# A split GELU gate on one core: a small 16-partition load issued ahead of the first store on ScalarE's queue

## The chip, the core and the metric

The kernel runs on one core of a Trainium2 chip. The metric is the device time of one execution in microseconds (us), the median over the runs shown; lower is better. The core has engines that take their own instructions in order: ScalarE (ACT in the profile), VectorE (DVE), GpSimd (POOL), SyncE (SP), TensorE (PE). SP and ACT each feed a DMA queue (q1 and q10 in this profile), and 16 DMA engines move what both queues hold.

## What is computed

The input is split in two halves along its last dimension; the first half goes through the exact GELU and is multiplied by the second.

```python
x = np.random.randn(32, 512, 2048).astype(np.float32)
x1, x2 = x[..., :1024], x[..., 1024:]
out = (0.5 * x1 * (1 + erf(x1 / np.sqrt(2)))) * x2
```

134.22 MB are read and 67.11 MB are written, and each element is used once.

## The kernel before

The 16,384 rows are cut into 16 tiles of 1,024 rows: 128 partitions with 8 rows each. One tile's input takes 64 KB of each partition (8 MB in all), its output 32 KB (4 MB in all). There are two input buffers `x0`, `x1` and two output buffers `o0`, `o1`; tile i uses number i % 2.

Everything is ordered by hand, with semaphores. `load` (L49) issues a load on SP's queue. `store` (L56) waits until VectorE has done all multiplies issued so far (`mul_done`) and then issues a store on the queue that it is given. Ahead of the loop ScalarE issues `opening` (L63), a load of 512 bytes to each of 8 partitions of a scrap tile; SP issues the load of tile 0 in two halves of 4 rows (semaphores `first[0]` and `first[1]`) and that of tile 1 whole.

In the loop over tiles, each tile is worked in steps of rows: (0,5) and (5,8), and for the first and the last tile (0,2), (2,4) and (4,8). Each step is one GELU on ScalarE (L87), from the input buffer to the output buffer, and one multiply on VectorE (L95) in the output buffer. After the steps the store of the tile goes out on ScalarE's queue (q10) and the load of tile i + 2 on SP's (q1). Tile 0 is stored in two halves of 4 rows, 16 KB per partition each: the first half as soon as its second step is multiplied (`hi == 4`), the second at the end of the tile. The store of tile 14 and the two half stores of tile 15 go out on SP's queue instead, and count on `tail_stored`.

The load of tile i + 2 and the store of tile i count on the same semaphore, `ready[i % 2]`, 16 for each. ScalarE waits for it once ahead of a tile's first GELU, so that a tile begins when its input has landed and the store that last used its output buffer has landed too:

```python
            if i == 0 and lo % 4 == 0:
                nc.scalar.wait_ge(first[lo // 4], 16)
            elif lo == 0:
                nc.scalar.wait_ge(ready[k], n[ready[k].name])
```

At the end ScalarE waits for `opened` (the scrap load), and SP waits for `tail_stored` (L125), which is the last instruction.

Of the kernel before, what the change touches and what calls it, by code (L numbers as in the profile page):

```python
# [1 line left out]

# [4 lines left out]

GELU = mybir.ActivationFunctionType.Gelu


@with_exitstack
def kernel(
    ctx: ExitStack,
    tc: tile.TileContext,
    x: bass.AP,
    out: bass.AP,
):
    nc = tc.nc
    P = nc.NUM_PARTITIONS

    x_flat = x.flatten_outer_dims()
    out_flat = out.flatten_outer_dims()
    n_rows, dim = x_flat.shape
    half = dim // 2

    R = 8
    x_t = x_flat.rearrange("(n p r) d -> n p r d", p=P, r=R)
    o_t = out_flat.rearrange("(n p r) d -> n p r d", p=P, r=R)
    n_tiles = x_t.shape[0]
    x_bufs = [nc.alloc_sbuf_tensor(f"x{k}_tile", [P, R, dim], x.dtype) for k in range(2)]  # L30
    o_bufs = [nc.alloc_sbuf_tensor(f"o{k}_tile", [P, R, half], out.dtype) for k in range(2)]

    first = [nc.alloc_semaphore(f"first{j}") for j in range(2)]
    ready = [nc.alloc_semaphore(f"ready{k}") for k in range(2)]
    gelu_done = nc.alloc_semaphore("gelu_done")
    mul_done = nc.alloc_semaphore("mul_done")
    tail_stored = nc.alloc_semaphore("tail_stored")
    opened = nc.alloc_semaphore("opened")  # L40
    scrap = nc.alloc_sbuf_tensor("scrap_tile", [8, 128], x.dtype)
    n = {sem.name: 0 for sem in [*first, *ready, gelu_done, mul_done, tail_stored, opened]}

    def counted(ins, sem, by):
        ins.then_inc(sem, by)
        n[sem.name] += by

    def load(i, rows, sem):
        ins = nc.sync.dma_start(out=x_bufs[i % 2][:, rows, :], in_=x_t[i][:, rows, :])  # L49
        counted(ins, sem, 16)  # L50
        return ins

    def store(queue, i, rows, sem):
        queue.wait_ge(mul_done, n[mul_done.name])
        counted(
            queue.dma_start(out=o_t[i][:, rows, :], in_=o_bufs[i % 2][:, rows, :]), sem, 16  # L56
        )

    opening = nc.scalar.dma_start(out=scrap[:, :], in_=x_t[0][:8, 0, :128])  # L63
    counted(opening, opened, 16)
    for ins in (
        opening,
        load(0, slice(0, 4), first[0]),
        load(0, slice(4, 8), first[1]),
        load(1, slice(0, 8), ready[1]),
    ):  # L70
        tc.no_tile_sem_insts.add(ins.ins.name)
    tc.close()
    tc.compile()  # L73

    for i in range(n_tiles):
        k = i % 2
        last = i == n_tiles - 1
        pieces = i == 0 or last
        steps = ((0, 2), (2, 4), (4, 8)) if pieces else ((0, 5), (5, 8))
        for lo, hi in steps:  # L80
            rows = slice(lo, hi)
# [4 lines that stand above are left out]
            counted(  # L86
                nc.scalar.activation(  # L87
                    out=o_bufs[k][:, rows, :], in_=x_bufs[k][:, rows, :half], func=GELU
                ),
                gelu_done,  # L90
                1,
            )
            nc.vector.wait_ge(gelu_done, n[gelu_done.name])
            counted(
                nc.vector.tensor_mul(  # L95
                    out=o_bufs[k][:, rows, :],
                    in0=o_bufs[k][:, rows, :],
                    in1=x_bufs[k][:, rows, half:],
                ),
                mul_done,  # L100
                1,
            )
            if pieces and hi % 4 == 0:
                if last:
                    store(nc.sync, i, slice(hi - 4, hi), tail_stored)
                else:
                    store(nc.scalar, i, slice(hi - 4, hi), ready[k])
        if not pieces:
            if i == n_tiles - 2:
                store(nc.sync, i, slice(0, R), tail_stored)  # L110
            else:
                store(nc.scalar, i, slice(0, R), ready[k])
        if i + 2 < n_tiles:
            nc.sync.wait_ge(mul_done, n[mul_done.name])
            load(i + 2, slice(0, R), ready[k])


    nc.scalar.wait_ge(opened, 16)
    nc.scalar.drain()  # L119
    for sem in (*first, *ready, opened):  # L120
        nc.scalar.sem_clear(sem)
    nc.vector.drain()
    nc.vector.sem_clear(gelu_done)
    nc.sync.sem_clear(mul_done)
    nc.sync.wait_ge(tail_stored, n[tail_stored.name]).then_inc(  # L125
        tail_stored, -n[tail_stored.name]
    )


# [1 line left out]
_INS = ['x']  # L131
_OUTS = [((32, 512, 1024), 'float32')]


# [23 lines left out]
```

## Time and profile before

| | |
|---|---|
| time, median of 3 runs | 469.23 us (469.21 to 469.29) |
| profiled execution, first to last instruction (span) | 467.8 us |
| median less span, outside the first and last instruction | 1.4 us |
| VectorE busy | 140.5 us, 34 multiplies |
| ScalarE busy | 115.5 us, 34 GELUs and one table load |
| HBM traffic | 201.3 MB, 430 GB/s over the span |
| DMA packets | 5,057 |

The profile gives the profiled execution's span and no separate device time for it; the three timed runs lie within 0.08 us of one another. Times in the views are counted from the first instruction. "ACTq" and "SPq" mark DMA issues by ScalarE and SyncE, which are not counted as busy. The trace also holds one record for each DMA packet: its start, its queue, how long it took and its bytes. It does not name the DMA engine, but on one engine a packet begins when the one before it ends, so that the records can be strung together into 16 rows.

### The profile page before, as it was taken

The page shows a single profiled execution, that of the slowest core. Times are in us where ns is not written, and L with a number is a line of the kernel's source. Part 1 is how long each engine was busy: PE and PEld are TensorE (multiplying, and loading weights), DVE is VectorE, ACT ScalarE, POOL GpSimd, SP SyncE. Part 2 cuts the span into 40 slices and gives each one's busy share as a digit, 9 for nine tenths or more (in the row PEclk, how much of TensorE's full clock was granted, in tenths as well). Part 3 has the DMA queues.
Part 4 walks back from the last instruction along what each step waited for, and adds up shares of the span by engine and source line. Part 5 has one row for each costly group of instructions (what it writes and reads, how often), then busy time and mean ns, then how long its engine had stood idle before and what let it go on. Part 6 is the DMA issues. An engine that isn't in the chain of part 4 may idle for free.

```text
span 467.8 us, 154 instructions
## 1 busy us (share of the span) xinstructions
DVE 140.5 (30%) x34; ACT 115.5 (25%) x35; POOL 0.2 (0%) x4
## 2 busy tenths in 40 slices
DVE  0330515207051060511606115060150702507043
ACT  1320606041060410604105050050501506014060
POOL 0000000000000000000000000000000000000000
DMA  8999999999999999999999999999999999999988
GB/s 359 448 448 448 398 406 496 403 403 448 459 437 403 440 412 493 403 403 448 487 409 403 445 406 493 403 403 448 493 403 403 448 426 471 403 426 426 493 384 379
DMA packets 5057, 201.34 MB, mean 430 GB/s; under 512 B 568, under 2 KB 576, under 8 KB 576
## 3 DMA queue, kind: packets, MB, share of 16 engines
q1 hardware_dynamic: 2880, 142.61, 70.6%
q10 hardware_dynamic: 2176, 58.73, 29.1%
q14 instruction: 1, 0.01, 0.0%
HBM read 134.22 MB, written 67.11 MB: 430 GB/s over the span
## 4 chain that ended last, share of the span: by engine, by line
DMA 76%; DVE 14%; ACT 8%; ACTq 0%; SPq 0%; issue 0%
DMA out_dram<-o_tile 66%; DVE o_tile L95 14%; DMA x_tile<-in_x_dram 10%; ACT o_tile L87 8%; ACTq L119 0%; SPq L49 0%
## 5 line engine op out<-in xcount | busy, mean ns | idle before, releaser
L95 DVE TENSOR_TENSOR o_tile<-o_tile,x_tile 128x5120 f32<-128x5120 f32 (+3 forms) x34 | 140.5, 4171 | 319.7 <-ACT o_tile L87 319.7
L87 ACT ACTIVATE o_tile<-x_tile 128x5120 f32<-128x5120 f32 (+3 forms) x34 | 114.3, 3407 | 337.3 <-DMA out_dram<-o_tile 301.8
L87 ACT ACT_TABLE_LOAD x1 | 1.3, 1283 | 2.9 <-PEq L73 2.9
L142 POOL MEMSET const-bfloat16-1.0<- 128x1 bf16 x1 | 0.1, 102 | 0.0
L142 POOL MEMSET const-uint8-127<- 128x1 uint8 x1 | 0.1, 101 | 0.0
L142 POOL MEMSET const-float32-0.0<- 128x1 f32 x1 | 0.1, 99 | 0.2 <-issue 0.2
L142 POOL MEMSET const-float32-1.0<- 128x1 f32 x1 | 0.1, 98 | 0.0
## 6 DMA issues: line engine op xcount, KB each, us to landing
out_dram<-o_tile ACTq DMA_DIRECT2D x13, 4096.0 KB, 44.7
x_tile<-in_x_dram SPq DMA_DIRECT2D x2, 4096.0 KB, 16.7
out_dram<-o_tile ACTq DMA_DIRECT2D x2, 2048.0 KB, 34.4
out_dram<-o_tile SPq DMA_DIRECT2D x1, 4096.0 KB, 25.2
out_dram<-o_tile SPq DMA_DIRECT2D x2, 2048.0 KB, 7.8
x_tile<-in_x_dram SPq DMA_DIRECT2D x15, 44.4
scrap_tile<-in_x_dram ACTq DMA_DIRECT2D x1, 4.0 KB
```

The source lines that it names most:

```text
L87: nc.scalar.activation(out=o_bufs[k][:, rows, :], in_=x_bufs[k][:, rows, :half], func=GELU),
L95: nc.vector.tensor_mul(out=o_bufs[k][:, rows, :], in0=o_bufs[k][:, rows, :], in1=x_bufs[k][:, rows, half:],),
L142: nc = _bacc.Bacc("TRN2", target_bir_lowering=False, num_devices=1)
```

## The change

ScalarE issues one more small load, `herald`: 512 bytes to each of 16 partitions of a second scrap tile, which nothing reads. It is issued in tile 0, after the same wait for `mul_done` that the first store makes, directly ahead of that store and on the same queue. It counts on `opened`, and the wait for `opened` at the end is raised from 16 to 32.

```diff
     scrap = nc.alloc_sbuf_tensor("scrap_tile", [8, 128], x.dtype)
+    herald = nc.alloc_sbuf_tensor("herald_tile", [16, 128], x.dtype)
...
                 else:
+                    if hi == 4:
+                        nc.scalar.wait_ge(mul_done, n[mul_done.name])
+                        counted(
+                            nc.scalar.dma_start(
+                                out=herald[:, :], in_=x_t[0][:16, 0, :128]
+                            ),
+                            opened,
+                            16,
+                        )
                     store(nc.scalar, i, slice(hi - 4, hi), ready[k])
...
-    nc.scalar.wait_ge(opened, 16)
+    nc.scalar.wait_ge(opened, n[opened.name])
     nc.scalar.drain()
```

## The prediction

> **What bounds the kernel.** I read the page first, then the chain of waits, then the timeline at both ends, and last the single DMA packet records. A change counts here as measurable from 0.2%, 0.94 us.
>
> ```profile
> DMA  8999999999999999999999999999999999999988
> ...
> q1 hardware_dynamic: 2880, 142.61, 70.6%
> q10 hardware_dynamic: 2176, 58.73, 29.1%
> ...
> DMA 76%; DVE 14%; ACT 8%; ACTq 0%; SPq 0%; issue 0%
> ```
>
> The DMA engines are busy from the second slice to the last, and the two queues' packets fill 99.7% of 16 engines' span. The packet records say how full that is: 65,536 bytes take 2,418 ns, so 201.33 MB over 16 engines take 12.58 MB / 27.1 GB/s = 464.3 us. First packets start at 1.7 us, and the last end at about 467.0 on most engines. So only some 1.0 us is not filled: 0.6 in the first 4 us (the first packets are slow: 1.6 to 2.1 us for 32 KB, later 1.21), 0.36 between 20 and 40 us, around the first store. This is the most that a better start could give.
>
> The chain of waits names DVE and ACT, but between tiles both have time. A tile begins when two transfers have landed, and 13.3 us later its store and the next load are issued, while the queues still hold more than 15 us of older work (29.0 us per tile less 13.3). Only at the end is that cover short:
>
> ```profile
> 403.75 44.74 DMA out_dram<-o_tile
> 448.49 0.02 issue
> 448.51 1.91 ACT o_tile L87
> 450.42 1.80 ACTq L119
> 452.22 3.52 ACT o_tile L87
> 455.73 0.02 issue
> 455.76 4.42 DVE o_tile L95
> ```
>
> Tile 15 begins at 448.51, released by the store of tile 13, issued at 403.75. That is the line to watch.
>
> ```profile
> 454.97 0.34 SPq L56 DMA_DIRECT2D out_dram<-o_tile  x1
> ...
> 460.21 0.33 SPq L56 DMA_DIRECT2D out_dram<-o_tile  x1
> ```
>
> These (the timeline of the last stretch) are the issues of the two last half stores. In the packet records store 14 fills q1 from 447.6 to 457.28; the first half runs 457.28 to 462.14, the second from 462.14 to 467.0. So the first is issued 2.31 us before the engines come free for it, the second 1.93 us. An issue takes time to become packets:
>
> ```profile
> 0.73 0.59 ACTq L63 DMA_DIRECT2D scrap_tile<-in_x_dram  x1
> 0.73 1.33 SPq L49 DMA_DIRECT2D x_tile<-in_x_dram  x3
> ```
>
> Issued at 0.73, these show first packets at 1.69 and 1.74, after 0.96 and 1.01 us. With 1.0 us the true slack is 1.3 and 0.9 us. The kernel is bound by bytes, with an end that tolerates about 0.9 us of delay.
>
> **What sets the order of the packets.** One engine's records, strung by start and end, around the first store (issued by ScalarE at 19.26):
>
> ```
> start   queue  ns    bytes
> 20.50   q1    1213   32768   last packet of load 0, second half
> 21.71   q1       9       4   its semaphore
> 21.71   q1    2674   65536   load 1, packet 1
> 24.38   q10    611   16384   store, packet 1
> 24.99   q1    2460   65536   load 1, packet 2
> 27.45   q10    611   16384   store, packet 2
> ...
> 43.29   q1    2418   65536   load 1, packet 8
> 45.70   q10    611   16384   store, packet 8
> 46.31   q1       9       4   semaphore of load 1
> 46.32   q10      9       4   semaphore of the store
> 46.32   q1    2418   65536   load 2, packet 1
> ```
>
> All 16 engines do this. While both queues hold work, they take strict turns, one record each, and a 4-byte semaphore record takes a turn like a 64 KB packet. A load has 8 packets and a semaphore per engine, and so has a store; from 24.4 us on the queues run in step, and each pair (load i + 2, store i) ends together at each tile. At the end too: semaphore of load 15 at 447.57, of store 13 directly behind it, then store 14.
>
> **The change part by part.**
> - The bytes: on each engine one 512-byte packet (25 ns in the opening load's records) and a semaphore (9 ns): 0.03 us. It is on the path, since nothing else is free.
> - ScalarE's time: one more issue, between 0.36 (the stores') and 0.59 us (the opening's) ahead of the store; I take 0.4, a 16-engine transfer as the stores are. The store is issued at 19.66. Behind it on ScalarE stands the GELU of rows 4 to 8, which waits for its load until 22.47: 2.8 us of cover, so nothing. The extra wait has the store's own value and is met at the same moment. SP and POOL are not passed.
> - `opened` at 32: awaited at the end, by 448 us; the herald lands by 30 or so. Nothing.
> - The 0.25 us that load 1's packet 1 takes over 2,418 ns, with the store arriving behind it: the trace does not show whether the store's arrival or the first 64 KB packet causes it. Between -0.36 (all of the hole near the first store goes) and +0.27 (it is paid twice); I take 0.
> - The turns. The herald is issued when the store was, at 19.26, so I let it take the store's turn at 24.38. Then, per engine: herald, load 1 packet 2, herald's semaphore, load 1 packet 3, store packet 1. The store has been waiting by then. **q10 has lost two turns to q1**, and since both queues never run empty until the end, it never gets them back.
>
> In mid kernel this costs nothing: loads end two store packets earlier, stores two load packets (4.8 us) later, a tile starts 4.9 us later, against 15.7 us of cover. The cover being gone, each us would cost one; it is not near.
>
> At the end it costs. The two turns are filled with store 14's 32 KB packets, 1.21 us each: the semaphore of store 13 comes 2 x 1.21 + 0.03 = 2.45 us later. ScalarE starts tile 15 at 450.96. The half stores are issued at 457.42 and 462.66. The engines are through with store 14 at 457.3, as before, and the first half's packets are there at 458.4: 1.1 us idle. They run to 463.3. The second half's come at 462.66 + 1.0 = 463.65, run 4.86 us to 468.5, and land 0.45 us later (as 467.34 to 467.81 now): 468.97 against 467.81, **+1.16 us**. That is the lower end: it lets an idle queue's first packet take no longer than others. Upper end: load 0's first half, alone on its engines, landed 12.04 us after issue with 9.68 us of packets, 2.36 us of overhead; so the second half lands by 462.66 + 4.86 + 2.36 = 469.88, +2.07. That row is an HBM read, the second half follows its sister on the queue nearly without a gap; I take a value near the lower end, +1.3. Span 467.8 + 1.3 = 469.1; with 1.4 outside the span (the median lies 1.4 above it), **470.5 us**.
>
> [...]
>
> **Rivals.**
> 1. Lag of one turn: the herald's data and semaphore share one, being 512 and 4 bytes. For it: the opening load's 8 semaphores follow their data after 21 ns. Against: load packets had perhaps not arrived then, and under contention each record above takes its own turn. Tile 15 starts 1.24 us late; the second half is issued at 461.45, its packets are there at 462.45 instead of 462.17: +0.3 us, up to +0.86 by the 2.36 us of overhead. 469.5 us.
> [...]
> 3. More than two turns, if the store also comes too late for its turn. Three: tile 15 starts 3.67 us late, the second half is issued at 463.88, lands 6.3 us later: 470.2, +2.4; 471.6 us.
> 4. Faster by over 0.94 us needs nearly all of the 1.0 us of holes, of which 0.6 lies before the herald's issue: no row gives it.
>
> **How the numbers follow.** Two turns 0.55; one turn 0.20; none 0.16; three or more, or another delay, 0.06; faster by a way that I do not see 0.03. Of the two-turn case nearly all lies over 0.94 us (lower end 1.16, less up to 0.36 if the hole goes): I count 0.50 of it; with the last delay, slower 0.56. Same: 0.20 + 0.16 + 0.05 = 0.41. Range 469.2 (no turn lost) to 471.3 (two turns, upper end): it leaves out three turns and the gain.
>
> **What would show it.** Right: in the packet records the first store's packet 1 near 29.2 instead of 24.4, with one 512-byte and one 4-byte q10 record ahead of it on each engine, a load packet between; tile 2 starting near 76.3 (71.40 before), tile 1 near 45.8 (47.02); tile 15 near 450.96; SP's last issues near 457.4 and 462.7; a hole of about 1 us in the DMA at 457.3. Wrong: tile 15 at 448.5 or 449.8, or engines free of holes at the end. The prediction falls if the herald's two records do not cost q10 two turns, or if an issue becomes packets in much less than 1.0 us at the end.

## The result and the profile after

The changed kernel takes 471.21 us, median of 5 runs (470.84 to 471.36); the kernel before, beside it, 469.25. The ratio is 1.0039 (95% interval 1.0028 to 1.0050). The span grew from 467.8 to 469.9 us.

The page after, its DMA rows and the shares of its chain. They look like those of before: a slice is 11.7 us wide, and the holes that matter are under 1 us.

```profile
DMA  8999989999999999999999999999999999999998
...
q1 hardware_dynamic: 2880, 142.61, 70.5%
q10 hardware_dynamic: 2208, 58.73, 29.0%
...
DMA 76%; DVE 14%; ACT 8%; ACTq 0%; SPq 0%; issue 0%
```

q10 has 32 packets more (2,208 against 2,176): 16 of data, 16 semaphores. The chain of waits, its last pieces (start, length, what):

```profile
409.26 42.28 DMA out_dram<-o_tile
451.54 0.02 issue
451.56 1.91 ACT o_tile L88
453.47 1.80 ACTq L129
455.27 3.52 ACT o_tile L88
458.79 0.02 issue
458.81 4.42 DVE o_tile L96
```

Tile 15 now begins at 451.56, 3.05 us later than the 448.51 of before, and still on the landing of store 13. The rest of the chain has kept its lengths. SP's issues of the two last half stores, from the timeline:

```profile
458.03 0.34 SPq L57 DMA_DIRECT2D out_dram<-o_tile  x1
...
463.26 0.33 SPq L57 DMA_DIRECT2D out_dram<-o_tile  x1
```

They too are 3.06 and 3.05 us late. What that leaves empty is seen by cutting out two short stretches (columns: stretch, its length, busy time of DVE, ACT and POOL with the number of instructions, PE clock, share of the DMA engines' time, GB/s). In the kernel after:

```profile
458.45:458.85 0.40, 0.04 (x1) 0.33 (x1) 0.00 (x0) 1.00 0.00 0
463.50:464.00 0.50, 0.00 (x0) 0.00 (x0) 0.00 (x0) 1.00 0.02 0
```

No data packet begins in either. In the kernel before, near the same places, the engines are busy:

```profile
458.00:458.80 0.80, 0.80 (x1) 0.00 (x0) 0.00 (x0) 1.00 0.91 389
463.50:464.00 0.50, 0.00 (x0) 0.00 (x0) 0.00 (x0) 1.00 0.92 393
```

Where the lag comes from stands in the packet records. One engine around the first store, strung as in the prediction:

```
start   queue  ns    bytes
21.83   q1       9       4   semaphore of load 0, second half
21.84   q1    2418   65536   load 1, packet 1
24.25   q10     27     512   herald
24.27   q1    2418   65536   load 1, packet 2
26.69   q10      9       4   semaphore of the herald
26.70   q1    2844   65536   load 1, packet 3
29.54   q10    611   16384   store, packet 1
...
41.64   q10    611   16384   store, packet 5
42.24   q1    3000   65536   load 1, packet 8
45.24   q10    611   16384   store, packet 6
45.85   q1       9       4   semaphore of load 1
```

All 16 engines do this: their heralds start at 24.10 to 24.58, the store's first packets at 29.42 to 30.00. The herald takes the turn that the store had, its 4-byte semaphore the next one, and the store begins at 29.5 instead of 24.4. At the end (another stretch of one engine) the two lost turns are filled with store 14:

```
445.82  q1       9       4   semaphore of load 15
445.83  q10   1213   32768   store 13, packet 7
447.04  q1    1213   32768   store 14, packet 1
448.25  q10   1213   32768   store 13, packet 8
449.46  q1    1213   32768   store 14, packet 2
450.67  q10      9       4   semaphore of store 13
```

To size holes and slow packets I add up, over the 16 engines, the time that the data packets would take at 2,418 ns for 64 KB and in proportion, with the 4- and 512-byte records as they are, and take it from the time elapsed ("lost time", per engine). Up to 455 us, before tile 15 stores anything, 2.46 us are lost before the change (1.7 of them ahead of the first packet) and 3.14 after it: 0.68 more. From 455 to 466 us 0.06 are lost before and 1.31 after: 1.25 more, at the end. Together this is 1.93 of the 2.04 us by which the span grew.

### The profile page after: what moved, and what is told of

The parts are those of the page before. It is cut to its first block, busy times and chain, and to the rows that moved or that the text cites. A ratio compares the mean times of both kernels' runs of the same rounds, so it can differ in the third digit from the quotient of the medians.

```text
span 469.9 us, 155 instructions
## 1 busy us (share of the span) xinstructions
DVE 140.5 (30%) x34; ACT 115.5 (25%) x35; POOL 0.2 (0%) x4
## 3 DMA queue, kind: packets, MB, share of 16 engines
q10 hardware_dynamic: 2208, 58.73, 29.0%
## 4 chain that ended last, share of the span: by engine, by line
DMA 76%; DVE 14%; ACT 8%; ACTq 0%; SPq 0%; issue 0%
DMA out_dram<-o_tile 66%; DVE o_tile L96 14%; DMA x_tile<-in_x_dram 10%; ACT o_tile L88 8%; ACTq L129 0%; SPq L50 0%
```

## The experiments

The theory ("turns"): q10 loses two turns to q1 and never gets them back (its "lag" is the number of turns lost); at the end two packets of store 14 run ahead of store 13's semaphore, tile 15 starts late and the engines wait for its half stores. The rivals: the extra read or the slowed packets near the first store cost the time; or the later issue of that store does. Times are medians; the kernel before took 469.29 to 469.33 beside these runs.

### Is it the end? Store 14 moved off SP's queue

```diff
             if i == n_tiles - 2:
-                store(nc.sync, i, slice(0, R), tail_stored)
+                store(nc.scalar, i, slice(0, R), tail_stored)
```

With the herald:

> The change with the store of tile 14 on ScalarE's queue behind store 13, instead of SP's. Theory of turns: q10 still lags two turns, but when load 15 is through nothing stands in q1, so store 13 ends without store 14's packets ahead of it: tile 15 starts 448.5 to 449.2, no idle DMA at the end, 469.3 to 470.0 us. Rival (time lost near the first store, not at the end): 471.2 as the changed kernel.

469.79 us (one of eleven runs took 471.14). Its chain of waits:

```profile
408.94 39.90 DMA out_dram<-o_tile
448.84 0.02 issue
448.86 1.91 ACT o_tile L88
```

and the stretch that was empty in the changed kernel:

```profile
458.45:458.85 0.40, 0.40 (x1) 0.00 (x0) 0.00 (x0) 1.00 0.95 410
```

The issue of store 13 is as late as in the changed kernel (408.94 against 409.26), so the two turns are lost here too. But nothing stands in q1 after load 15; tile 15 starts at 448.86 and the hole is gone, and with it 1.4 of the 1.9 us. The other 0.5 stays. The control, the same edit without the herald:

> The kernel before with only the store of tile 14 moved to ScalarE's queue; the control of the run before it. Theory of turns: no turn is lost, tile 15 starts at 448.5, the same bytes follow: 469.2 to 469.4 us. Rival (moving store 14 gains by itself): under 468.3.

469.27 us against 469.29 (ratio 1.000, 0.9991 to 1.0008), tile 15 at 448.69. Moving store 14 gains nothing by itself; it only takes away the herald's effect at the end.

### Is the end's slack so short? Tile 15 started late, no herald

```diff
+            if last and lo == 0:
+                nc.scalar.wait_ge(mul_done, n[mul_done.name])
+                nc.scalar.activation(
+                    out=x_bufs[0][:, 0:3, :896], in_=x_bufs[k][:, 0:3, :896], func=GELU
+                )
```

> No herald. Ahead of tile 15's first GELU ScalarE does an extra GELU of 3 x 896 elements per partition into the input buffer that is free, about 2.4 us, so that tile 15's own work starts about 2.35 us late with the queues untouched. If the end has about 0.9 us of slack, as the theory has it: the last half store is issued at 462.56 and lands 6.59 us later, 469.15 in the span: 470.5 us (470.3 to 470.7). Rival (the end is not where the time goes): 469.2 to 469.4.

470.55 us. The queues are those of before until then (the wait ahead of tile 15 ends at 448.62, 0.1 us later); from the timeline of ScalarE and SP:

```profile
448.62 2.44 ACT L88 ACTIVATE x_tile<-x_tile 128x2688 f32<-128x2688 f32 x1 [21.89 <-DMA out_dram<-o_tile]
450.97 7.20 ACT L92 ACTIVATE o_tile<-x_tile 128x2048 f32<-128x2048 f32 x3
...
462.65 0.33 SPq L56 DMA_DIRECT2D out_dram<-o_tile  x1
```

A start of tile 15 that is 2.46 us later than before (450.97 against 448.51) costs 1.25 us: 1.2 us are absorbed, a little more than the 0.9 that the prediction allowed.

### Is it the turns, and how many? Other heralds

Two partitions instead of 16 (`herald[2, 128]` from `x_t[0][:2, 0, :128]`):

> The herald with 2 partitions instead of 16, so 2 packets in all. Theory of turns: the engines that carry them lose two turns, and every wait is for all 16 engines, so tile 15 starts as late as in the changed kernel, near 451, less any slow packets: 470.4 to 471.2 us. Rival (cost in proportion to the bytes or engines of the herald): 469.3 to 469.6.

471.02 us. In the packet records two engines carry the herald, and only they have the store two turns late; tile 15 starts at 451.30. Two late engines of 16 cost 1.7 us where 16 cost 1.9, since every wait is for 16. This speaks against a cost by bytes.

The same 16 packets read from the output buffer instead of HBM (`in_=o_bufs[0][:16, 0, :128]`):

> The herald reads its 512 bytes from 16 partitions of the output buffer on the chip instead of from HBM; its place, queue and packets are the same. Theory of turns: as the changed kernel, 470.8 to 471.4 us, tile 15 near 451.0 to 451.6. Rival (the extra HBM read ahead of the first write disturbs the transfers): 469.3 to 470.0.

470.99 us. The extra HBM read is not the cause.

32 partitions, so three turns (`herald[32, 128]`):

> The herald with 32 partitions: two data packets and a semaphore on each engine, three turns. Theory of turns: a turn of lag takes 3.63 us of a cover of 13.8 us (29.0 a tile, less 15.2 from a load's end to the next load's packets), so three turns hold and four did not; tile 15 starts 3.67 us and some 0.6 of slow packets later than before, 452.7; the last half store is issued near 464.4 and lands 6.59 us later, 471.0: 472.4 us. Rival (the cost was the extra read near the first store): 471.2 to 471.4.

472.23 us (472.06 to 472.28). The timeline of ScalarE, then of SP:

```profile
452.41 3.71 ACT L88 ACTIVATE o_tile<-x_tile 128x2048 f32<-128x2048 f32 x2 [18.27 <-DMA out_dram<-o_tile]
```

```profile
464.11 0.33 SPq L57 DMA_DIRECT2D out_dram<-o_tile  x1
```

Tile 15 starts 0.85 us later than with two turns, and the run takes 1.0 us more; 1.21 was expected for the third turn, but less is lost to slow packets here (2.90 us by 455, against 3.14 in the changed kernel). A turn more costs about its packet.

Two heralds on ScalarE's queue, so four turns (the herald's lines a second time, into a tile of its own):

> Two heralds on ScalarE's queue. Theory of turns: four turns lost; tile 15 starts 4 x 1.21 + 0.07 = 4.9 us later than before plus up to 0.6 of slow packets, 453.4 to 454.0; the last half store is issued near 465.1 to 465.7 and lands 6.59 us after its issue as in the changed kernel, 471.7 to 472.3 in the span: 473.1 to 473.7 us, 2.4 us over the changed kernel. Rival (extra reads or a later issue of the store, 0.4 us each): 471.5 to 472.0.

Missed: 471.46 us, four of six runs between 470.88 and 471.85, two at 473.72 and 473.80. The profiled run shows why it can be less. In the records of the first store four turns are lost, as meant. But load 4 is issued late (timeline of SP; the kernel before issues it at 84.7, beside its store):

```profile
94.80 24.56 SPq L51 DMA_DIRECT2D x_tile<-in_x_dram  x2
```

In the records load 3 ends on q1 half a microsecond later, before load 4's packets are there, and q10 runs three of its packets in a row where one would be its turn; from there on the lag is two turns. Load 4's first packets start at 98.8 to 99.3 on the 16 engines, and q10 still takes a turn at 97.6 to 98.1, at least 2.8 us after the issue: beside a busy queue an issue took longer to count than the 1.0 us of the prediction. (Whether its packets come later or the engine chooses its next record early, the run does not tell.) The chain ends as with one herald:

```profile
408.98 42.32 DMA out_dram<-o_tile
451.30 0.02 issue
451.32 1.91 ACT o_tile L89
```

The cover, the time that a queue still has older work when its next transfer is issued, is 13.8 us by the prediction's terms: 29.0 a tile, less 0.9 to land, 13.3 to compute and 1.0 from issue to packets; with 2.8 us for the last it is 12.0. A turn of lag uses 3.63 us of it (2.42 + 1.21). So three turns (10.9) fit, and a fourth (14.5) does not. The two runs near 473.7 lie near the 473.1 to 473.7 us expected of four turns; there is no trace of either, so that they kept four turns is not shown.

### The other queue

The herald issued by SP instead (`nc.sync` in place of `nc.scalar` in its lines):

> The herald goes out on SP's queue at the same moment, behind load 1. Theory of turns: q1 loses two turns to q10 instead, and at the end nothing of store 14 runs ahead of store 13, since both loads and store 14 stand in one queue: tile 15 starts near 448.6 (before 448.51), end and time as before, 469.2 to 469.6. Rival (the extra read, or the packets slowed around it, cost the time wherever it is issued): 470.8 to 471.3.

470.40 us (469.49 to 470.52; two of eleven runs, 469.49 and 469.52, in the range expected): the median fits neither. The records show the turns as expected, q1 two behind, and no hole in front of the half stores from a wait for store 13. But one engine ran late. Landings of load 15 in the profiled run come between 448.13 and 448.46 on 15 engines, and at 449.62 on the last; in the kernel before the last engine is some 0.3 us behind the middle one. Tile 15 waits for it (the chain puts the wait down to the store that counts on the same semaphore):

```profile
406.25 43.37 DMA out_dram<-o_tile
449.62 0.02 issue
449.64 1.91 ACT o_tile L88
```

That engine also ends last, its last landing at 469.08 where the others' come by 468.08, and this is the time. It falls behind mostly between 100 and 190 us; why is open. Both heralds, one on each queue:

> Two heralds, one on ScalarE's queue as in the change and one on SP's. Theory of turns: two turns lost and two won back, tile 15 near 448.6 to 449.3, time 469.3 to 470.0 (0.07 us of packets, up to 0.6 of slow packets as seen in the changed kernel). Rival (the extra reads cost): at least 471.2.

469.74 us: taking back two turns takes back 1.5 of the 1.9 us, within the range expected. In the profiled run, which is longer than the median (span 470.4), 15 engines have q1 and q10 in step again; one has its packets 2 us late, from slow 64 KB packets between 30 and 45 us, and tile 15 waits for it (451.14). Three turns lost and two won back:

> A herald of 32 partitions on ScalarE's queue and one of 16 on SP's: three turns lost, two won back. Theory of turns: tile 15 starts 1.21 us later plus 0.2 to 0.6 of slow packets, which uses up the slack of the last half store (0.9 us): 469.6 to 470.2 us, up to 471 where one engine falls behind as in the run with two heralds on two queues. Rival (extra reads cost, three of them now): 471.5 or more.

477.90 us, far outside both theories. The lag at the end is one turn, as meant, but the time goes elsewhere: between 150 and 420 us the 64 KB load packets lose 4.5 us per engine on average, up to 0.79 us on one packet and mostly in the 10 us after a load has ended. In the traces before and after the change they lose 0.006 us per engine there (at most 2,436 and 2,498 ns for one), and the 32 KB store packets lose nothing in this run. This run says nothing on the price of one turn. Its cause is open.

### The issue and the place

No herald, but the first store issued as late as behind it, by a GELU of 256 elements into a scrap tile:

> No herald; a small GELU of 256 elements per partition into the scrap tile, waited for, delays the issue of the first store by 0.4 to 0.8 us. Theory of turns: the store keeps its turn or, if late for it, loses one; 469.2 to 469.5 us. Rival (the later issue of the store costs the time): 470.8 or more.

469.24 us (ten of eleven runs by 469.58, one at 471.57). The issue of the store, from the timeline:

```profile
19.69 0.38 ACTq L57 DMA_DIRECT2D out_dram<-o_tile  x1
```

It is as late as in the changed kernel (19.70), the store keeps its turn (its first packets start at 24.5 to 24.9) and tile 15 starts at 448.54. A later issue costs nothing. And the herald's load directly behind the opening load:

> The same 16-partition load, issued directly behind the opening load at the start instead of ahead of the first store. Theory of turns: nothing else waits in q10 then, so no turn is lost to q1 that matters; 469.2 to 469.5 us, tile 15 near 448.5. Rival (a load on all 16 engines from ScalarE's queue costs by itself): 470.8 or more.

469.37 us against 469.29 (ratio 1.0001, 0.9993 to 1.0010), tile 15 at 448.52. The same load costs nothing where no store waits behind it on its queue.

No version here beats the kernel before: it leaves some 1 us beyond the first packets' start unfilled, and none of the edits won any of it.

## Why the prediction was right

It forecast 470.5 us, slower by two lost turns that come due at the end; measured were 471.21, slower, and the lost turns and the late end are in the records. The size is less well founded: the measured median lies only 0.1 us under the upper end of the range, and that end was set by 2.36 us of overhead on the last half store, which measured 1.73 (6.59 from issue to landing less 4.86 of packets). What carried the time up there is mostly a term that was put at nothing (below). That 471.21 still fell into the range is partly luck.

- **Bound by bytes, with a short slack at the end.** Held. 2.46 us of delay without a herald cost 1.25, so the slack is 1.2 us (0.9 predicted). The store's packets followed their issue by 0.84 us (458.03 to 458.87) where 1.0 was taken, and the first of them on an idle queue took 0.616 us against 0.611: none of the extra 0.4 to 0.85 us of the load's first packets, so the lower end was the right one to lean on.
- **Strict turns, one record each, semaphore included.** Held to the record: herald at 24.25, its semaphore at 26.69, the store at 29.54 (29.2 predicted); tile 2 starts at 76.85 (76.3 predicted). A lag of one turn, the first rival, was not seen: on each engine a packet of load 1 lies between the herald and its semaphore.
- **Free in mid kernel.** Held for two and three turns: by 455 us the time lost is 3.14 and 2.90 us, against 2.46 before, and with two turns the difference is lost near the first store (the mis-sized term below). Four used up the cover, which the prediction counted too loosely: a lag makes the load end earlier as well as the store later (two turns, on a middle engine and with 0.7 us of slow packets in both: load 1's semaphore at 45.91 instead of 46.40, that of the first store at 51.96 instead of 46.40), so that by the packets' times a turn costs 3.63 us of cover and not 2.42, and in the run with four turns an issue beside a busy queue took at least 2.8 us to count, not 1.0.
- **ScalarE's time, the later issue.** Nothing, as predicted (469.24 for the delay alone).
- **The end.** 2.45 us from two turns, predicted; the start of tile 15 moved by 3.05. By issue and landing: the last half store is issued 3.05 us later and lands 6.59 us after its issue instead of 7.60, so +2.04. With 2.45 alone it would be +1.44, against the 1.3 taken and the 1.16 of the lower end. The missing 0.28 us comes mainly from a slip in the sum: its 0.45 us of landing, counted from 467.34, were added to the end of a middle engine, and before the change a middle engine ended at 467.06, 0.75 us ahead of the last landing.
- **The mis-sized term** is the 0.25 us hole at load 1's packet 1, bounded between -0.36 and +0.27 and taken as 0. The time lost there came out 0.68 us higher, outside these bounds, mostly by a second hole that the prediction did not foresee. The first hole did not stay or go: it moved to load 1's packet 3, ahead of the store's new place, grew to 0.45 us, and a second of 0.57 us appeared at load 1's packet 8 (means of the 16 engines; 2,844 and 3,000 ns on the one above). With the old hole gone, the net up to 455 us is the 0.68 us of lost time; with store 14 moved, so that the end costs nothing, 0.5 us is what remains of the slowdown. That the first hole goes with the start of the first store, not with the first 64 KB packet, is seen in the changed kernel, where packets 1 and 2 take 2,418 ns; with three and four turns the slow packet moves on with the store, to 29 and 32 us. What makes packet 8 slow was not found. It is slow too when the herald reads no HBM; with a herald on two engines it is not, but there packets 2 and 3 take some 2.6 us on most of the other engines.
- That no turn is lost, 0.16 in the prediction, did not happen: in the changed kernel the herald comes behind load 1's packet 1 on every engine (24.10 to 24.58 against 21.69 to 22.17), and no run with the herald at this place on ScalarE's queue has it ahead.

## What to carry to other kernels

In the records before and after the change two DMA queues that both held work alternated record by record. A transfer of one 512-byte packet (27 ns) and a semaphore (9 ns) per engine cost its queue two turns, each as long as the other queue's packet: 2.42 us beside the load, 1.21 beside store 14. Its bytes said nothing about its price: 1.7 us for 2 packets, 1.9 for 16. The lag was free in mid kernel, where the waits had some 12 us of cover (the estimate above), and came due at the end, with 1.25 of the 1.93 us. So I would look there first: at which transfer the last tile waits for, and what the other queue puts in front of it. A wait for all 16 engines followed the latest of them: two touched engines held tile 15 back from 448.51 to 451.30, sixteen to 451.56.

## What was not expected of the hardware

- 64 KB load packets slowed down on all 16 engines at once, by 0.45 and 0.57 us in the mean on single packets near the first store of the changed kernel, and by 4.5 us per engine over 270 us in the run with three turns lost and two won back, while the 32 KB store packets kept 1,213 ns. Whether the order of turns matters for it was not shown: no run isolates it.
- Single engines fell behind the other 15, by 1.2 us (herald on SP's queue) or 2 us (on both), and stayed there; tile 15 then waited for that one (449.64 and 451.14).
